# Splitting the operands of both head sums one stage ahead of their products

## The chip, the cores and the metric

The kernel runs on one core of one Trainium2 chip. The metric is the time of one execution on the device, in microseconds (us); of several runs the median is given. TensorE multiplies matrices (PE in the profile; PEld is its weight load), VectorE (DVE), ScalarE (ACT) and GpSimd (POOL) work elementwise, and SyncE (SP) issues the DMAs. Each engine takes its instructions in one fixed order, written when the program is built; an instruction that waits holds up everything behind it on its engine.

## What is computed

One layer over 1024 tokens of width 1024: a retention mixer (4 heads) and an RWKV-7 mixer (8 heads of 64 channels) read one projection; then come an output projection, a gated FFN, an embedding gate and a norm. The change touches two sums over the 64 channels of an RWKV head:

```python
kk = k * k_k.reshape(H, N)
kk = kk * lax.rsqrt(jnp.maximum(jnp.sum(kk * kk, axis=-1, keepdims=True), 1e-24))
k = k * (1.0 + (a - 1.0) * k_a.reshape(H, N))
...
bonus = jnp.sum(r * k * r_k, axis=-1, keepdims=True) * v
return (y + bonus.reshape(B, S, W)) * g
```

## The kernel before

Channels lie on the partitions and tokens run along the free dimension, in two halves of 512 tokens. The dense layers are long rows of 128x512 matmuls (tile `d` and, in the tail, `pd` and `pg`). Each fp32 operand is split into two parts, `hi` (rounded on ACT, L250) and `lo` (the rest, subtracted on DVE or POOL, L251), and a product is hi by hi, hi by lo and lo by hi.

The RWKV mixer works on eight groups: four pairs of heads, p0 to p3, for the first half of the tokens and then again for the second. A group (`rwkv_group`) goes through the stages prep, ops, A, tok, mid, chain, fin and done. `weave` writes the program: whenever the dense matmuls written so far are worth the wait that a stage has asked for, it writes the group's next step, and otherwise one more piece of the dense layer. A group enters tok when the group before is in fin, so the two run beside each other. A list scheduler then fixes each engine's order: by the order of writing where it can, and later where an operand or a buffer is not yet free by its reckoning.

The steps that matter here:

- prep squares k times its weight into `kk2`; ops sums it over the channels with two matmuls against a block of ones (tile `ss`).
- A makes `kp` (r times k times a weight, L615), the masked products `pb`, and a chain of 62 small DVE instructions on `tmp` and `R` (L646, L648: 31 pairs, shapes 128x8x31 down to 128x8x1) that inverts a triangular block. That chain is called the inversion here.
- tok makes two sets of `pk` products and from them `aak` on DVE (L668), sums `kp` over the channels (tile `bo`, L672), multiplies the sum by v into `bv` (L674), and transposes five operands on PE (tile `pq`, four transposes each), each set copied out by four ACT copies (L685).
- fin of the group before transposes `Y` into `py`, normalises it on DVE into `yn` (L779) and transposes back (`pyt`). L784 adds `bv`.

`headsum` splits its operand into a tile `hs` pair and multiplies in one go. Its `hi` half takes one of the two buffers of tag "f" (HBUF = 2), which `Y` and `yn` of the group before use as well; its `lo` half takes one of the five of tag "t". The PSUM tiles `ss`, `bo`, `pq`, `pk`, `pb` and `pS` share the two banks of `psa`.

Of the kernel before, what the change touches and what calls it, by code (L numbers as in the profile page):

```python
# [178 lines left out]
def tile_hybrid_layer(ctx: ExitStack, tc: tile.TileContext, I, out):  # L179
# [7 lines left out]
    def mm(ps, lhsT, rhs, start, stop, more=False):  # L187
        n = math.prod(rhs.shape[1:])
        pe[0] += n / 2.4 if rhs.dtype == F32R else 2 * max(107.0, n / 1.2)
        m = nc.tensor.matmul(ps, lhsT, rhs, start=start, stop=stop, skip_group_check=more)  # L190
        tail["mm"] = m.ins
        return m
# [22 lines left out]
    def K(n):  # L215
        return cst[:, _C[n][0]:_C[n][1]]
# [4 lines left out]
    def pv(i):  # L221
        return par[:, i:i + 1]
# [3 lines left out]
    def psa(name):  # L226
        return psr.tile([P, 512], F32, tag="ra", name=name, bufs=2)

    def psq(name):
        return psd.tile([P, 512], F32, tag="d", name=name)  # L230
# [3 lines left out]
    def pse(name):  # L234
        tag = ("ra", "rc", "ra", "rm", "rt")[npx[0] % 5]
        npx[0] += 1
        return psr.tile([P, 512], F32, tag=tag, name=name, bufs=2 if tag == "ra" else 1)
# [11 lines left out]
    def split(src, hi, lo, eng=None):  # L249
        act(hi, src, AF.Copy)  # L250
        return (eng or V).tensor_tensor(out=lo, in0=src, in1=hi.bitcast(F32), op=ALU.subtract)  # L251
# [101 lines left out]
    with ExitStack() as s1:  # L353
# [194 lines left out]
        def v3(t):  # L548
            return t.rearrange("p (u t) -> p u t", t=C)

        def flat(t):
            return t.rearrange("p h t -> p (h t)")
# [3 lines left out]
        def rwkv_group(p, hf):  # L556
# [6 lines left out]
            def tt2(name):  # L563
                return t2.tile([P, HS], F32, tag="t", name=name)
# [1 line left out]
            def tf(name):  # L566
                return t2.tile([P, HS], F32, tag="f", name=name, bufs=HBUF)

            def headsum(ps, t):

                hi, lo = (t2.tile([P, HS], F32R, tag=HTAG[i], name="hs", bufs=(HBUF, 5)[i]) for i in range(2))
                split(t, hi, lo)
                mm(ps, onesr, hi, start=True, stop=False)
                mm(ps, onesr, lo, start=False, stop=True)

# [2 lines left out]
                dma(out=t, in_=lowd[4 * i + p, :, tok])  # L578
            kk2 = tt2("kk2")
            act(kk2, k, AF.Square, scale=pv(KK + p))  # L580
            yield "prep", PREPW

            ss = psa("ss")
            headsum(ss, kk2)
            behind = tc.issue_after(invs[-1]) if invs else nullcontext()
            with behind:
                V.tensor_scalar(out=th, in0=th, scalar1=1.0, scalar2=None, op0=ALU.add)
# [23 lines left out]
            kp = tt2("kp")  # L611
# [47 lines left out]
            XR = rp.tile([P, NU, 2, C], F32, tag="XR", name="XR")  # L659
            KA = rp.tile([P, NU, 2, C], F32, tag="KA", name="KA", bufs=KAB)  # L660
            aak = v3(tt2("aak"))
            for g in range(2):
                us = slice(4 * g, 4 * g + 4)
                pk = psa("pk")
                for u in range(4):
                    mm(pk[:, u * P:(u + 1) * P], flat(kabd[:, 4 * g + u]), AR[:, :, 4 * g + u, :], start=True, stop=True)
                pkv = pk.rearrange("p (u x t) -> p u x t", u=4, x=2)
                V.tensor_tensor(out=aak[:, us, :], in0=pkv[:, :, 0, :], in1=K("mak").unsqueeze(1).broadcast_to([P, 4, C]), op=ALU.mult)  # L668
                V.tensor_tensor(out=KA[:, us, 1, :], in0=pkv[:, :, 1, :], in1=mincl4, op=ALU.mult)
                yield "tok", 900  # L670
            bo = psa("bo")
            headsum(bo, kp)  # L672
            bv = t2.tile([P, HS], F32, tag="bv", name="bv", bufs=1)
            V.tensor_tensor(out=bv, in0=bo, in1=v, op=ALU.mult)  # L674
            SG = t2.tile([P, HS], F32, tag="sg", name="sg", bufs=1)
# [14 lines left out]
            for h in range(2):  # L690
                lo, up = slice(C * h, C * h + 32), slice(C * h + 32, C * h + C)
# [51 lines left out]
            for u in range(NU):  # L743
# [5 lines left out]
                if hf == 0 or u < NU - 1:  # L749
# [3 lines left out]
                    ps = psa("pS")[:, 0:P]  # L753
# [543 lines left out]
        for h in range(2):  # L1297
            for k in range(KT):
                tasks[f"mix{h}{k}"] = (mix_load(h, k), 0, ["wo0" if h else "x0free", f"ret{k}{h}" if k < 4 else f"group{k - 4}{h}"])
        weave([(f"group{p}{hf}", rwkv_group(p, hf), need[p]) for hf in range(2) for p in range(4)],  # L1300
              tasks, dg, count, pe, done)

# [142 lines left out]
    for a, b in passes:  # L1445
        h, n = a // HS, b - a
        t = slice(a - h * HS, b - h * HS)
        for d in range(KT):
# [9 lines left out]
            ps = psq("pg")[:, 0:n] if a < HS else pse("pg")[:, 0:n]  # L1458
# [86 lines left out]
```

## Time and profile before

| | |
|---|---|
| median of 3 runs | 1598.35 us (1597.43 to 1599.26) |
| the profiled execution, its own time | 1598.74 us |
| its span, first to last instruction | 1597.0 us |
| PE, DVE, ACT, POOL busy | 94%, 75%, 45%, 32% of the span |
| mean granted TensorE clock | 0.986 of 2.4 GHz |
| chain that ended last, by engine | PE 57%, DVE 23%, ACT 7%, DMA 6% |

The span is the stretch that the trace shows; the time of the run lies 1.74 us above it. The chain that ended last is followed back from the last instruction, at each step to what released it. The groups of the RWKV mixer lie between about 75 and 915 us; the FFN's second half and the embedding gate come after them.

### The profile page before, as it was taken

The page shows a single profiled execution, that of the slowest core. Times are in us where ns is not written, and L with a number is a line of the kernel's source. Part 1 is how long each engine was busy: PE and PEld are TensorE (multiplying, and loading weights), DVE is VectorE, ACT ScalarE, POOL GpSimd, SP SyncE. Part 2 cuts the span into 40 slices and gives each one's busy share as a digit, 9 for nine tenths or more (in the row PEclk, how much of TensorE's full clock was granted, in tenths as well). Part 3 has the DMA queues.
Part 4 walks back from the last instruction along what each step waited for, and adds up shares of the span by engine and source line. Part 5 has one row for each costly group of instructions (what it writes and reads, how often), then busy time and mean ns, then how long its engine had stood idle before and what let it go on. Part 6 is the DMA issues. An engine that isn't in the chain of part 4 may idle for free.

```text
span 1597.0 us, 21675 instructions
## 1 busy us (share of the span) xinstructions
PE 1497.2 (94%) x7328; PEld 1220.0 (76%) x7328; DVE 1203.1 (75%) x2466; ACT 722.4 (45%) x1442; POOL 512.7 (32%) x389
## 2 busy tenths in 40 slices
PE   6999899998888889989889999999999999999997
PEld 5777768776677767767768877778888888888897
DVE  7668895969889696894875545768888888886675
ACT  6755435353545647445344324543333333334554
POOL 7411111121321122324223340455555555570000
PEclk9999999999999999999999999999999999999998
DMA  6544242242544555335233546332223222331222
GB/s 199 175 154 166 96 129 84 89 152 78 174 133 145 189 165 190 96 105 155 87 127 113 171 119 188 115 121 85 92 90 90 91 93 86 119 93 56 83 91 75
DMA packets 108767, 194.09 MB, mean 122 GB/s; under 512 B 12272, under 2 KB 16496, under 8 KB 108656
## 3 DMA queue, kind: packets, MB, share of 16 engines
q1 hardware_dynamic: 108656, 192.71, 38.0%
q8 instruction: 58, 0.95, 0.2%
q14 instruction: 53, 0.43, 0.1%
HBM read 151.24 MB, written 41.42 MB: 121 GB/s over the span
## 4 chain that ended last, share of the span: by engine, by line
PE 57%; DVE 23%; ACT 7%; DMA 6%; issue 4%; POOL 2%; SPq 0%; ACTq 0%; DVEq 0%; POOLq 0%
PE d L190 31%; PE pd L190 13%; PE pg L190 6%; DVE tmp L646 4%; DVE R L648 3%; DMA st<-in_w_gate_dram 2%; POOL lo L251 2%; DMA st<-in_w_up_dram 1%; DVE lo L251 1%; ACT hi L250 1%; DVE Dm L640 1%; DVE inv L599 1%; PE pkh L190 1%; PE pb L190 1%; ACT BA L685 1%
## 5 line engine op out<-in xcount | busy, mean ns | idle before, releaser
L190 PE MATMUL d<-hT,hi 128*128 128x512 f32 x1408 | 452.0, 401 | 4.1 <-ACT hi L250 4.1
L251 POOL TENSOR_TENSOR lo<-st,hi 128x512 fp32r<-128x512 f32 x173 | 241.8, 1399 | 590.6 <-ACT hi L250 531.3
L190 PE MATMUL d<-x,hi 128*128 128x512 f32 x960 | 319.7, 408 | 8.9 <-ACT x L339 8.0
L190 PEld LDWEIGHTS d<-hT,hi 128*128 128x128 f32 x1408 | 263.5, 192 | 54.9 <-ACT hi L250 5.6
L250 ACT ACTIVATE hi<-st 128x512 fp32r<-128x512 f32 x298 | 187.0, 628 | 258.2 <-PE d L190 96.4
L190 PE MATMUL d<-hT,lo 128*128 128x512 f32 x704 | 279.8, 398 | 5.9 <-DVE lo L251 3.4
L190 PE MATMUL pd<-ring 128*128 128x512 f32 x948 | 260.4, 389 | 0.0
L190 PEld LDWEIGHTS d<-x,hi 128*128 128x128 f32 x960 | 177.1, 192 | 43.3 <-ACT x L339 8.0
L190 PEld LDWEIGHTS pd<-ring 128*128 128x128 f32 x948 | 177.9, 188 | 37.1 <-ACT rm L1145 0.2
L190 PE MATMUL d<-x,lo 128*128 128x512 f32 x480 | 192.9, 402 | 2.8 <-POOL lo L251 2.4
L190 PEld LDWEIGHTS d<-hT,lo 128*128 128x128 f32 x704 | 134.2, 191 | 38.3 <-DVE lo L251 6.3
L251 DVE TENSOR_TENSOR lo<-st,hi 128x512 fp32r<-128x512 f32 x125 | 115.7, 927 | 55.9 <-ACT hi L250 54.9
L1147 DVE TENSOR_TENSOR x<-x,pd 128x512 f32<-128x512 f32 x180 | 118.6, 679 | 26.9 <-PE pd L190 26.9
L251 POOL TENSOR_TENSOR ring<-xr,ring 128x512 fp32r<-128x512 f32 x53 | 73.2, 1386 | 146.5 <-ACT ring L250 67.3
L250 ACT ACTIVATE ring<-rm 128x512 fp32r<-128x512 f32 x87 | 53.8, 629 | 131.3 <-DVE rm L1080 83.8
L190 PEld LDWEIGHTS d<-x,lo 128*128 128x128 f32 x480 | 92.0, 192 | 23.1 <-POOL lo L251 4.7
L646 DVE TENSOR_TENSOR tmp<-Dt,R 128x248 f32<-128x248 f32 (+30 forms) x248 | 89.5, 361 | 3.2
L648 DVE TENSOR_TENSOR R<-R,tmp 128x248 f32<-128x248 f32 (+30 forms) x248 | 83.8, 338 | 3.3
L190 PE MATMUL d<-mix,hi 128*128 128x512 f32 x256 | 82.1, 400 | 0.9 <-ACT hi L250 0.9
L251 DVE TENSOR_TENSOR ring<-rm,ring 128x512 fp32r<-128x512 f32 x65 | 58.4, 902 | 13.0 <-ACT ring L250 12.1
L250 ACT ACTIVATE ring<-xr 128x512 fp32r<-128x512 f32 x57 | 34.9, 625 | 73.8 <-PE pd L190 72.6
L190 PEld LDWEIGHTS d<-mix,hi 128*128 128x128 f32 x256 | 48.1, 192 | 10.8 <-ACT hi L250 1.3
(315 smaller groups left out, 2393.7 us busy)
## 6 DMA issues: line engine op xcount, KB each, us to landing
st<-in_w_gate_dram SPq DMA_DIRECT2D x88, 256.0 KB, 2.9
st<-in_w_up_dram SPq DMA_DIRECT2D x88, 256.0 KB, 2.9
st<-in_w_in_dram SPq DMA_DIRECT2D x86, 256.0 KB, 2.9
xr<-in_w_down_dram SPq DMA_DIRECT2D x44, 256.0 KB, 2.7
retd<-rt SPq DMA_DIRECT2D x32, 256.0 KB, 2.5
rr<-retd SPq DMA_DIRECT2D x32, 256.0 KB, 3.4
st<-in_w_o_dram SPq DMA_DIRECT2D x32, 256.0 KB, 3.0
rkvd<-rkvt SPq DMA_DIRECT2D x24, 256.0 KB, 2.1
```

What stands on the lines that cost most here:

```text
L190: m = nc.tensor.matmul(ps, lhsT, rhs, start=start, stop=stop, skip_group_check=more)
L250: act(hi, src, AF.Copy)
L251: return (eng or V).tensor_tensor(out=lo, in0=src, in1=hi.bitcast(F32), op=ALU.subtract)
L599: V.reciprocal(out=inv, in_=inv)
L640: V.tensor_tensor(out=Dm, in0=d0v[:, 0].rearrange("p u t -> p t u").unsqueeze(2).broadcast_to([P, 32, 4, NU]), in1=d0v[:, 1].rearrange("p ...
L646: V.tensor_tensor(out=tmp[:, :, 0:i], in0=Dt[:, i:i + 1, 0:i].broadcast_to([P, 8, i]), in1=R[:, :, i:i + 1].broadcast_to([P, 8, i]), op=AL ...
L648: V.tensor_tensor(out=R[:, :, 0:i], in0=R[:, :, 0:i], in1=tmp[:, :, 0:i], op=ALU.subtract)
L685: act(dst(h)[h * C:(h + 1) * C, j::2, :], pqv[j * C:(j + 1) * C, :, h, :], AF.Copy)
L1147: V.tensor_tensor(out=dst, in0=dst, in1=ps, op=ALU.subtract if name == "P4" else ALU.add)
```

## The change

`headsum` is cut in two. `headparts` allocates the two halves and splits; `headsum` only multiplies. The split of `kk2` is written at the end of prep instead of in ops, and the split of `kp` at the beginning of tok, ahead of the two sets of `pk`, instead of behind them. No operation is added or taken away.

```diff
-            def headsum(ps, t):
-
+            def headparts(t):
                 hi, lo = (t2.tile([P, HS], F32R, tag=HTAG[i], name="hs", bufs=(HBUF, 5)[i]) for i in range(2))
                 split(t, hi, lo)
+                return hi, lo
+
+            def headsum(ps, hi, lo):
+
                 mm(ps, onesr, hi, start=True, stop=False)
                 mm(ps, onesr, lo, start=False, stop=True)
...
             act(kk2, k, AF.Square, scale=pv(KK + p))
+            kk2 = headparts(kk2)
             yield "prep", PREPW
 
             ss = psa("ss")
-            headsum(ss, kk2)
+            headsum(ss, *kk2)
...
             aak = v3(tt2("aak"))
+            kp = headparts(kp)
             for g in range(2):
...
             bo = psa("bo")
-            headsum(bo, kp)
+            headsum(bo, *kp)
```

The scheduler turns this into other orders. Lines below the edit carry numbers that are 3 to 5 higher in the changed kernel. On PE, in tok of p1 in the first half, the order before has the transposes of the group before first and the sum and the five sets behind them:

```order
L196 MATMUL pyt<-cst,yn 128x128 x4
L190 MATMUL d<-x_98,hi 128x512 x2
L190 MATMUL d<-x_98,lo 128x512
L190 MATMUL d<-x_98,hi 128x512
L190 MATMUL bo<-hs,onesr 128x512
L196 MATMUL pq<-cst,aak 128x128 x4
L190 MATMUL d<-x_98,hi 128x512
L190 MATMUL d<-x_98,lo 128x512
L190 MATMUL bo<-hs,onesr 128x512
L190 MATMUL d<-x_98,hi 128x512 x2
L190 MATMUL d<-x_98,lo 128x512
L196 MATMUL pq<-cst,v 128x128 x4
```

In the changed kernel the sum comes nine dense matmuls behind the second set of `pk`, and the transposes of the group before come 36 dense matmuls after it, as before at the 681st dense matmul of the program:

```order
L190 MATMUL pk<-AR,kabd 128x128 x4
...
L190 MATMUL bo<-hs,onesr 128x512 x2
L190 MATMUL d<-x_98,hi 128x512 x2
L190 MATMUL d<-x_98,lo 128x512
L190 MATMUL d<-x_99,hi 128x512
L196 MATMUL pq<-cst,aak 128x128 x4
L190 MATMUL d<-x_99,hi 128x512
L190 MATMUL d<-x_99,lo 128x512
...
L196 MATMUL pyt<-cst,yn 128x128 x4
L196 MATMUL pq<-cst,AR 128x128 x4
```

So `bo` and four of the five `pq` sets moved ahead of `pyt`. Counted in dense matmuls, `bo` moves forward by 40, 54, 36, 51, 52, 49 and 49 in the seven groups that follow another; in the first group it stays. The `pq` sets move by 18 to 52. They now stand 4 to 19 dense matmuls behind `bo` and mostly 6 to 12 apart from each other (`aak` of p1 in the second half stands right behind `bo`). `pyt` itself stays where it was, or stands 9 to 13 dense matmuls earlier in three groups and 6 later in one.

On ACT, at the same place, the first fence is before and the second is the change. `Y` belongs to the group before, `hs<-kp` is the `hi` half, and L685 or L690 are the copies out of `pq`:

```order
L763 ACTIVATE Y<-pZ 128x4x64
L756 ACTIVATE Sn<-pS,PC 128x128
L250 ACTIVATE hi<-st 128x512 x2
L250 ACTIVATE hs<-kp 128x512
L685 ACTIVATE XR<-pq 64x4x64 x4
L580 ACTIVATE kk_2244<-k,par 128x512
L250 ACTIVATE hs<-kk_2244 128x512
```

```order
L768 ACTIVATE Y<-pZ 128x4x64
L250 ACTIVATE hs<-kp 128x512
L761 ACTIVATE Sn<-pS,PC 128x128
L756 ACTIVATE STb<-pZ 64x64
L250 ACTIVATE hi<-st 128x512
...
L690 ACTIVATE KA<-pq 64x4x64 x4
L250 ACTIVATE hs<-kk_2244 128x512
L690 ACTIVATE XR<-pq 64x4x64 x4
```

The rounding of `kp` moved from behind both `Y` copies to between them, and the rounding of the next group's `kk2` moved back behind the fourth set of `pq` copies.

On DVE, at the same place, `hs<-kp` is the `lo` half. Before, it stood behind the end of the inversion:

```order
L784 SCALAR_TENSOR_TENSOR Y<-pyt,par,bv 128x512
L652 COPY Xd<-tmp 128x256
L251 TENSOR_TENSOR hs<-kp,hs 128x512
L654 STREAM_TRANSPOSE R<-Xd 128x256
L785 SCALAR_TENSOR_TENSOR Y<-Y,par,sg 128x512
L674 TENSOR_TENSOR bv<-bo,v 128x512
```

In the changed kernel it stands inside the inversion, at its twelfth pair of 31:

```order
L650 TENSOR_TENSOR tmp<-Dt,R 128x8x21
L652 TENSOR_TENSOR R<-R,tmp 128x8x21
L650 TENSOR_TENSOR tmp<-Dt,R 128x8x20
L251 TENSOR_TENSOR hs<-kp,hs 128x512
L652 TENSOR_TENSOR R<-R,tmp 128x8x20
```

`bv` stays behind `Y<-pyt` (L784, now L789), because it has one buffer and that instruction reads the old one.

## Rows read from the trace of the kernel before

**Rows 1.** The page's first part: busy us, share of the span, instructions.

```profile
PE 1497.2 (94%) x7328; PEld 1220.0 (76%) x7328; DVE 1203.1 (75%) x2466; ACT 722.4 (45%) x1442; POOL 512.7 (32%) x389
```

**Rows 2.** Busy time by stretch: us, PE, PEld, DVE, ACT, POOL; clock, DMA.

```profile
60.00:960.00 900.00, 828.00 (x4235) 663.88 (x4234) 676.98 (x1717) 418.87 (x927) 221.12 (x170) 0.98 0.42 134
400.00:500.00 100.00, 87.75 (x472) 69.62 (x471) 87.50 (x244) 47.85 (x110) 24.96 (x18) 0.98 0.46 147
```

**Rows 3.** Waits of PE over the span: total us, times, longest us.

```profile
PE pS L196 <- DVE STb L752: 18.2, 22, 1.7
...
PE bo L190 <- DVE hs L251: 4.9, 3, 2.3
...
PE pyt L196 <- DVE yn L779: 1.9, 2, 1.0
PE pyt L196 <- DVE R L648: 1.8, 1, 1.8
PE pq L196 <- ACT Vbd L685: 1.6, 4, 0.6
...
PE pq L196 <- ACT BA L685: 1.5, 6, 0.4
PE ss L190 <- ACT KA L685: 1.4, 3, 0.5
...
PE bo L190 <- ACT hs L250: 1.3, 1, 1.3
...
PE pq L196 <- ACT XR L685: 0.5, 2, 0.3
```

**Rows 4.** Tile hs: ns min/median/max, first and last start; idle time before it.

```profile
L250 ACT ACTIVATE hs<-kp x8: 613/632/635, 110.2 to 816.6; 128x512 fp32r<-128x512 f32 x8
L251 DVE TENSOR_TENSOR hs<-kp,hs x8: 641/685/1762, 130.2 to 817.3; 128x512 fp32r<-128x512 f32 x8
...
  PE pyt L196: 12.2, 5
```

**Rows 5.** Timeline of ACT, p1, first half: start, us, instruction, [idle before <-releaser].

```profile
230.07 0.64 ACT L250 ACTIVATE hs<-kp 128x512 fp32r<-128x512 f32 x1 [4.01 <-PE pyt L196]
...
234.58 1.55 ACT L685 ACTIVATE Vbd<-pq 64x256 f32<-64x256 f32 x4
```

**Rows 6.** Timeline of PE, p1, second half.

```profile
592.84 0.63 PE L196 MATMUL pyt<-cst,yn 128*128 128x128 f32 x4 [1.03 <-DVE yn L779]
593.23 0.71 PE L190 MATMUL d<-mix,hi 128*128 128x512 f32 x2
...
595.66 0.50 PE L190 MATMUL bo<-hs,onesr 128*128 128x512 f32 x1 [1.26 <-ACT hs L250]
...
598.73 0.80 PE L190 MATMUL bo<-hs,onesr 128*128 128x512 f32 x1 [2.13 <-DVE hs L251]
```

**Rows 7.** Busy time by stretch, columns as in rows 2.

```profile
597.30:604.10 6.80, 5.37 (x15) 4.20 (x16) 4.66 (x8) 4.51 (x9) 0.00 (x0) 0.50 0.75 222
```

**Rows 8.** Timeline of DVE, p1, first half.

```profile
210.08 0.33 DVE L646 TENSOR_TENSOR tmp<-Dt,R 128x160 f32<-128x160 f32 x1
```

**Rows 9.** Timeline of PE at the same place: the first set of pk.

```profile
213.59 1.05 PE L190 MATMUL pk<-AR,kabd 128*128 128x128 f32 x8
```

**Rows 10.** Chain that ended last: start, us, what (six dense matmuls).

```profile
357.41 1.38 PE d L190 x6
```

**Rows 11.** Timeline of DVE: the second aak of p1 first, p2 second half.

```profile
220.44 0.40 DVE L668 TENSOR_TENSOR aak<-pk,cst 128x256 f32<-128x256 f32 x1
...
690.79 0.41 DVE L668 TENSOR_TENSOR aak<-pk,cst 128x256 f32<-128x256 f32 x1
```

**Rows 12.** Timeline of PE: dense matmuls beside the first of these.

```profile
219.96 0.62 PE L190 MATMUL d<-x,hi 128*128 128x512 f32 x2
```

**Rows 13.** Timeline of PE, p2 of the second half.

```profile
692.51 0.88 PE L190 MATMUL rY<-rr 128*128 128x128 f32 x4 [2.74 <-DVE rmisc L859]
```

**Rows 14.** Timeline of DVE, p1, second half: the second pb.

```profile
553.18 0.49 DVE L634 TENSOR_TENSOR d<-pb,cst 128x128 f32<-128x128 f32 x2 [8.72 <-PE pb L190]
```

**Rows 15.** Timeline of PE, p3, second half: two sets of transposes of the retention.

```profile
812.52 1.12 PE L196 MATMUL rtp<-cst,rr 128*128 128x128 f32 x4 [4.21 <-ACT rr L829]
```

## Prediction

> **What bounds the kernel now.** I begin with the page's first part [rows 1]: PE is busy 94% of the span, so a change that adds and removes no operation can only win or lose idle time of PE (or time in which its clock is down). The windows say where that idle time lies [rows 2]: from 60 to 960 us, where the eight groups of the RWKV mixer run beside dense matmuls, PE is busy 828.00 of 900 us, that is, 72 us idle. Behind that stretch the change moves no instruction. In the worst stretches DVE is as full as PE (87.50 of 100 us against 87.75), so DVE work that comes later there can hold PE up.
>
> The waits of PE [rows 3] then say on whom it waits: mostly on DVE's `STb` in the chain stage (`pS`, 18.2 us in 22 waits), which the change doesn't touch, and in the rows shown of tok and fin on `hs` (`bo`: 4.9 and 1.3 us), on `yn` and `R` (`pyt`: 1.9 and 1.8 us), and on the ACT copies of a set (`pq`: 1.6, 1.5 and 0.5 us; `ss`: 1.4 us).
>
> Why `bo` waits is seen in the tile `hs` and in two timelines. The `hi` half for `kp` takes a buffer of tag "f" that `yn` of the group before holds until `pyt` has read it. So ACT stands idle before it until `pyt`, 12.2 us in five groups [rows 4], 4.01 us of it in p1 of the first half [rows 5]. Only then comes `lo` on DVE, behind other work. In p1 of the second half PE waits 1.26 us for `hi` and 2.13 us for `lo` [rows 6], and straight behind that the granted clock is 0.50, the 1.2 GHz level, for 6.80 us, in which PE is busy 5.37 us [rows 7].
>
> **The change, part by part.** The sum is made against the profiled execution, 1598.74 us (0.39 us above the median of the runs).
>
> *The waits of `bo`.* In the changed order of p1 in the first half, `lo` stands behind the `tmp` that starts at 210.08 us [rows 8], and lasts about 0.69 us. `hi` takes 0.63 us on ACT [rows 4] and stands ahead of the second copy of `Y`, so it must be there by then too. `bo` is written behind both sets of `pk`, the first of which ran at 213.59 us [rows 9]. By these rows both halves are ready more than 2 us before PE can ask. Gain: 4.9 + 1.3 = 6.2 us, all of it.
>
> *The waits of `pyt`.* In most groups `pyt` keeps its place among the dense matmuls, but now `bo` and four sets of `pq` lie ahead of it. A set takes 0.39 us of PE [rows 6], `bo` some 0.5 us, so PE gets there about 2.1 us later relative to DVE. That covers the longest waits of 1.8 and 1.0 us in part or whole; I take 2.4 of the 3.7 us.
>
> *The waits between sets.* Four ACT copies of one set take 1.55 us [rows 5]; a dense matmul takes 1.38 / 6 = 0.23 us [rows 10]. The sets now stand mostly 6 to 12 dense matmuls, 1.4 to 2.8 us, apart, so that the copies mostly keep up. Of 1.6 + 1.5 + 0.5 = 3.6 us I take three quarters, 2.7. The wait of `ss` behind such copies, 1.4 us, goes because the sets are long over when `ss` comes.
>
> *The clock.* The lowered stretch of [rows 7] followed the waits of `bo`, 1.26 + 2.13 us within 4 us. Without them I take it to stay at 2.4 GHz: half of 5.37 us, 2.7 us. Whether the waits caused it, no row shows; the bounds are 0 and 2.7.
>
> Gains: 6.2 + 2.4 + 2.7 + 1.4 + 2.7 = 15.4 us.
>
> *New waits.* `lo` now takes its 0.69 us of DVE inside the inversion, ahead of `aak`, and nothing on DVE leaves that stretch in exchange. Before, the second `aak` of p1 in the first half ended at 220.44 + 0.40 = 220.84 us [rows 11], and PE was among dense matmuls from 219.96 to 220.58 us [rows 12]. Now `aak` ends near 221.5 us, and the set `pq<-aak`, moved to stand behind four or five dense matmuls after `bo`, is asked for at about 220.6 us. That is a wait of about 0.9 us; in p2 of the second half (690.79 us [rows 11]) it is as tight. I price it at 0.7 us (one `lo`) in five groups: 3.5 us. The bounds: 0, if DVE has room to catch up, as in p1 of the second half, where it stood 8.72 us waiting for `pb` [rows 14] and that set now comes earlier; and 2.74 us a time, the wait of PE on a late DVE in p2 of the second half [rows 13]. I lie nearer to the low end because the cause of the wait is one instruction of 0.7 us. What is queued behind a waiting `pq` on PE is the dense row and the next set; ACT's copies wait for that.
>
> In three groups `pyt` stands 9 to 13 dense matmuls earlier (2.1 to 3.0 us), about as much as the work that came ahead of it, while `yn` is 0.7 us later; in p2 and p3 of the first half I add 0.85 us each: 1.7 us.
>
> *Edits at nothing.* The split of `kk2` in prep: its rounding on ACT stands behind the fourth set of copies instead of beside them, and ACT is 45% busy. What covers it is the dense row between prep and `ss`. If that cover is short, `ss` waits one rounding and one subtraction, 0.63 + 0.69 = 1.3 us, a group. In some groups that rounding still needs the buffer that `pyt` frees; so ACT's 12.2 us shrink but don't vanish, and what is late next is the copies of the fifth set behind it. `bv` keeps its place; `bo` then holds a PSUM bank longer, which the other sets can do without as they go through the second bank. The bounds of this are 0 and 1.3 us a group; I take 0.
>
> Sum: 15.4 − 3.5 − 1.7 = 10.2 us, 1598.74 − 10.2 = **1588.5 us**.
>
> **A rule weighed.** The `lo` for `kp` takes 685 ns in the median, but 1762 ns once [rows 4]: something else held that one up for 1.08 us. The Trainium skill (SBUF — State Buffer, "Who interferes with whom") gives a cause: VectorE's second read port is shared with GpSimd as an exclusive lock, so a subtraction of two SBUF operands is blocked by a GpSimd instruction that reads SBUF. That would speak against putting it in a stretch where GpSimd is busy. By the trace, seven of eight were not held, and GpSimd is busy 221.12 of 900 us here [rows 2], so I leave the sum as it is and keep the lock as rival E.
>
> **The rivals.**
>
> *B. More is won.* PE comes into the later stages at other times relative to ACT and DVE. In p3 of the second half it waited 4.21 us for `rr` [rows 15]; if the five sets and `bo` lie ahead of that wait instead of behind it, most of it is filled. With the new waits (5.2 us) half gone as well: 1588.5 − 4.2 − 2.6 = 1581.7, and with another lowered stretch like that of [rows 7] avoided, 1.7 to 2.7 more: about 1580 us. Against it: `rr` and the dense rows around it keep their order.
>
> *C. No change.* DVE sets the pace where it is busy 87.50 of 100 us; it does the same work, and what PE wins in tok it gives back at the next `pS`. The 18.2 us there [rows 3] would grow by about 10. Time: about 1598 us. For it: `STb` is by far the largest wait. Against it: PE is just as full, and from 60 to 960 us DVE has 223 us free.
>
> *D. Slower.* `pq<-aak` stands too early: DVE is later than I reckon, PE waits in each of five groups as long as in [rows 13], 2.74 us, and loses to a lower clock behind it some 1.7 us (half of a stretch half as long as that of [rows 7]). That is 5 × 4.44 = 22.2 us in place of the 3.5 us of the sum: 1598.74 + 22.2 + 1.7 − 15.4 = 1607.2 us. It decides where the new waits at `pq` and `pyt` average over 15.4 / 7 = 2.2 us in each group that follows another. For it: the sets moved up by 18 to 52 dense matmuls while `aak` didn't get earlier on DVE. Against it: what precedes `aak` on DVE grew by a single instruction.
>
> *E. The subtraction is held.* In all seven moved groups `lo` takes the 1762 ns, 1.08 us more: 7.5 us on a DVE that leads to `aak`, `R` and `yn`. If three quarters of it reaches PE, 5.7 us, the time is 1588.5 + 5.7 = 1594.2 us. This is what that page's lock would do at its worst; this case's rows show it once in eight.
>
> *The change does nothing* can't be: the orders differ in every group after the first.
>
> **How the numbers follow.** Chances: the sum as reckoned 0.46 (its own range 1582 to 1594), B 0.12, C 0.18, D 0.16, E 0.08. The likeliest gives 1588.5 us. What this kernel's measurement can tell from no change is about 0.2%, 3.2 us: faster is below 1595.2, slower above 1601.5. The first case, B and E end below: 0.46 + 0.12 + 0.08 = 0.66; C within: 0.18; D above: 0.16. The range leaves out D and what of B lies beyond its estimate: 1579 to 1601 us, with about 0.2 outside.
>
> **What would show it right or wrong.** Right: no wait of PE on `hs` at `bo`; `hi` for `kp` on ACT without idle time until `pyt`; no lowered clock in p1 of the second half near 590 us; the wait of DVE for the second `pb` there gone; waits of `pq` on `aak` below 1 us each; PE's idle time from 60 to 960 us down from 72 to about 60 us. Wrong on the side of D: waits of `pq<-aak` of 2 us or more, with lowered clock behind them. On the side of C: `bo` without waits, but `pS` on `STb` well above 18.2 us. On the side of E: a median of `lo` near 1.7 us. The forecast also fails if `pyt` asks for `yn` so much earlier that its waits pass 3.7 us, or if `ss` now waits for its early split.

## The result and the profile after

The changed kernel takes 1592.16 us (median of 8 runs, 1587.93 to 1595.94) against 1602.54 us for the kernel before in runs beside it: a ratio of 0.9942 (95% interval 0.9922 to 0.9962), or 9.3 us less; the two medians are 10.4 us apart. The profiled execution took 1588.42 us, with a span of 1586.6 us against 1597.0. The forecast was 1588.5 us, 10.2 us less.

The page's first part reads nearly as in [rows 1]: the engines do the same work in a shorter span.

```profile
PE 1490.3 (94%) x7328; PEld 1218.7 (77%) x7328; DVE 1210.2 (76%) x2466; ACT 719.9 (45%) x1442; POOL 516.1 (33%) x389
```

The window that answers to the first of [rows 2] runs here from 59.51 to 942.51 us, between the same two PE instructions (`low<-rr` and `ryt`) that stood at 60.82 and 951.49 us before. Columns are as in [rows 2].

```profile
59.51:942.51 883.00, 815.26 (x4192) 657.16 (x4190) 677.96 (x1713) 413.45 (x923) 222.38 (x167) 0.98 0.42 135
```

PE is idle 883.00 − 815.26 = 67.7 us of it, where it was 72.0 us. Now the waits of PE, to be held against [rows 3] (total us, times, longest us):

```profile
PE pS L196 <- DVE STb L757: 18.9, 24, 2.3
...
PE ryt L196 <- ACT rr L876: 8.1, 3, 3.8
...
PE pq L196 <- ACT XR L690: 3.6, 6, 2.1
...
PE pq L196 <- DVE R L652: 2.2, 1, 2.2
PE pq L196 <- DVE KA L674: 1.6, 3, 0.9
...
PE bo L190 <- DVE KA L674: 0.7, 2, 0.5
...
PE ss L190 <- DVE hs L251: 0.6, 1, 0.6
PE pq L196 <- DVE tmp L650: 0.6, 1, 0.6
PE pq L196 <- ACT KA L690: 0.6, 2, 0.3
PE pq L196 <- ACT Vbd L690: 0.5, 2, 0.3
PE pq L196 <- ACT BA L690: 0.5, 2, 0.2
```

No wait of `bo` on `hs` is left and none of `pyt`. In their place stand waits of `pq` on DVE (2.2 + 1.6 + 0.6 = 4.4 us, one each in five groups), a longer wait of `pq` on ACT, and a longer one of the retention's `ryt`. The tile `hs` answers to [rows 4]: ACT no longer stands idle ahead of it until `pyt`.

```profile
L250 ACT ACTIVATE hs<-kp x8: 621/624/632, 108.8 to 779.3; 128x512 fp32r<-128x512 f32 x8
L251 DVE TENSOR_TENSOR hs<-kp,hs x8: 680/685/1759, 122.4 to 780.3; 128x512 fp32r<-128x512 f32 x8
...
  DVE hs L251: 1.7, 2
```

Where the time went is best seen by taking the same PE instruction in both traces and subtracting the starts (before minus after). Each column stands at such an instruction; its head is the start in the kernel before.

| us | 201 | 289 | 374 | 462 | 540 | 645 | 665 | 773 | 883 | 951 | 1587 |
|---|---|---|---|---|---|---|---|---|---|---|---|
| lead of the changed kernel | 1.31 | 3.63 | 6.24 | 8.91 | 8.77 | 9.99 | 13.44 | 8.95 | 8.96 | 8.99 | 9.62 |

The first 1.31 us arise before 61 us, ahead of any moved PE instruction, and 0.6 us after 951 us, where the orders are the same: those are the two executions, not the change. Of the rest, p1, p2 and p3 of the first half bring 2.3, 2.6 and 2.7 us, p1 of the second half 4.7 us (from 540 to 665 us), and p2 of the second half gives 4.5 us back.

### The profile page after: what moved, and what is told of

Its sections match the earlier page's. It is cut to its first block, busy times and chain, and to the rows that moved or that the text cites. A ratio compares the mean times of both kernels' runs of the same rounds, so it can differ in the third digit from the quotient of the medians.

```text
span 1586.6 us, 21684 instructions
## 1 busy us (share of the span) xinstructions
PE 1490.3 (94%) x7328; PEld 1218.7 (77%) x7328; DVE 1210.2 (76%) x2466; ACT 719.9 (45%) x1442; POOL 516.1 (33%) x389
## 4 chain that ended last, share of the span: by engine, by line
PE 63%; DVE 23%; DMA 5%; ACT 4%; issue 3%; POOL 2%; SPq 0%; DVEq 0%; ACTq 0%; POOLq 0%
PE d L190 36%; PE pd L190 14%; PE pg L190 6%; DVE tmp L650 3%; DVE R L652 3%; POOL lo L251 1%; DVE lo L251 1%; DVE Dm L644 1%; DVE inv L603 1%; PE pb L190 1%; DMA st<-in_w_up_dram 1%; DMA st<-in_w_gate_dram 1%; ACT hi L250 1%; PE pq L196 1%; PE pkh L190 1%
## 5 line engine op out<-in xcount | busy, mean ns | idle before, releaser
L652 DVE TENSOR_TENSOR R<-R,tmp 128x248 f32<-128x248 f32 (+30 forms) x248 | 87.4, 352 | 3.7
L650 DVE TENSOR_TENSOR tmp<-Dt,R 128x248 f32<-128x248 f32 (+30 forms) x248 | 84.2, 339 | 3.4
```

The costliest lines, as they stand in the source:

```text
L650: V.tensor_tensor(out=tmp[:, :, 0:i], in0=Dt[:, i:i + 1, 0:i].broadcast_to([P, 8, i]), in1=R[:, :, i:i + 1].broadcast_to([P, 8, i]), op=AL ...
L652: V.tensor_tensor(out=R[:, :, 0:i], in0=R[:, :, 0:i], in1=tmp[:, :, 0:i], op=ALU.subtract)
```

## The experiments

Ratios are to the kernel before, in runs beside each.

**Which half of the change.** `e1_kp_only` takes back the split of `kk2`:

```diff
-            kk2 = headparts(kk2)
             yield "prep", PREPW
 ...
-            headsum(ss, *kk2)
+            headsum(ss, *headparts(kk2))
```

> The changed kernel with the split of kk2 back in ops; only the split of kp stays early. Theory 1 (the whole gain comes from the split of kp, because PE no longer stands at bo and the pq sets come ahead of pyt): ratio to the kernel before 0.994 +- 0.002, PE's waits at bo below 1 us in all. Rival 2 (the early split of kk2 carries part of it, over ss and ACT): a ratio of 0.996 to 0.998. Rival 3 (most of the difference is run to run): 1.000.

Measured: 0.9934 (0.9916 to 0.9952). The orders on PE, ACT, DVE and POOL are those of the changed kernel, so the place where the split of `kk2` is written changes nothing there, and this run measures the same order a second time. PE waits 0.7 us at `bo`.

`e2_kk2_only` takes back the split of `kp`:

```diff
-            kp = headparts(kp)
             for g in range(2):
 ...
-            headsum(bo, *kp)
+            headsum(bo, *headparts(kp))
```

> The changed kernel with the split of kp back behind the two sets of pk; only the split of kk2 is early. PE's order is that of the kernel before. Theory 1: ratio 1.000 +- 0.001, the waits at bo as before, 6.2 us. Rival 2: 0.996 to 0.998, with the 1.4 us of ss gone and the idle time of ACT changed.

Measured: 1.0000 (0.9986 to 1.0014). Its waits of PE are those of [rows 3] again:

```profile
PE bo L190 <- DVE hs L251: 4.3, 4, 2.1
PE bo L190 <- ACT hs L250: 2.1, 2, 1.3
PE pyt L196 <- DVE yn L783: 2.0, 2, 1.1
PE pyt L196 <- DVE R L652: 1.8, 1, 1.8
```

So the gain comes with the split of `kp`; that of `kk2` brings nothing that these runs can tell (within 0.14%). Rivals 2 and 3 fall.

**Why bo was late.** `e3_before_rbuf` leaves the writing as it was and only gives the `hi` half of `kp` another buffer, that of `r`, which is free by then:

```diff
-            def headsum(ps, t):
+            def headsum(ps, t, tag="f", bufs=HBUF):
 ...
-            headsum(bo, kp)
+            headsum(bo, kp, "r", 1)
```

> The kernel before, with the split of kp where it was, but its hi half in the buffer of r (no longer needed there) instead of one that yn of the group before holds. In PE's order bo then moves forward by 35 to 56 dense matmuls without any change of the writing. Theory 1 in its narrow form (bo is late because hi has to wait for the buffer of yn; where the split is written does not matter): 0.994 to 0.996, ACT's idle time of 12.2 us before hi gone. Rival 4 (the place of the split is what counts): 0.999 to 1.001.

Measured: 0.9944 (0.9925 to 0.9963), the gain of the change within the noise. The scheduler now moves the split by itself. In the tile `hs` ACT's idle time until `pyt`, 12.2 us in [rows 4], is down to one wait:

```profile
L250 ACT ACTIVATE hs<-kp x8: 615/631/633, 109.0 to 727.7; 128x512 fp32r<-128x512 f32 x8
...
  PE pyt L196: 0.8, 1
```

So the cause is the buffer shared with `yn`. Writing the split earlier works because it then takes a buffer ahead of `yn`. The way there is not the same in every term: in this run `pq` waits 8.3 us on DVE, where the changed kernel waits 4.4.

`e4_before_bo_last` moves the sum and `bv` behind the five sets instead:

```diff
-            bo = psa("bo")
-            headsum(bo, kp)
-            bv = ...
 ...                                  (the five pq sets)
+            bo = psa("bo")
+            headsum(bo, kp)
+            bv = ...
```

> The kernel before, with the sum over kp and bv written behind the five pq sets instead of ahead of them; nothing is split earlier. In PE's order the sets come forward as in the changed kernel, and bo comes behind pyt by 5 to 15 dense matmuls. If the gain is in the sets having come forward and bo no longer standing ahead of them: 0.994 to 0.997. If it needs bo's operands early: bo waits again, 4 us or more, and the ratio is 0.998 to 1.001.

Measured: 0.9984 (0.9970 to 0.9998). The sets come forward, but `bo` waits again, in its waits of PE for 8.8 + 2.2 us, and the sets' first transposes wait for `aak`:

```profile
PE bo L190 <- DVE hs L251: 8.8, 4, 3.1
...
PE pq L196 <- DVE aak L668: 5.8, 6, 1.8
...
PE bo L190 <- ACT XR L681: 2.2, 1, 2.2
```

That is the second case. Moving the sets forward alone is worth little (0.16%); the operands of `bo` must be there too.

**Which groups.** The split of `kp` is early in one half of the tokens only, or everywhere but in p2 of the second half. The diff is that of e5; e6 has `hf == 1` in the same places, e7 and e11 `(p, hf) != (2, 1)`:

```diff
-            kp = headparts(kp)
+            if hf == 0:
+                kp = headparts(kp)
 ...
-            headsum(bo, *kp)
+            headsum(bo, *(kp if hf == 0 else headparts(kp)))
```

> The split of kp is early in the four groups of the first half of the tokens only. By the trace of the changed kernel PE's lead over the kernel before grows by 2.3, 2.6 and 2.7 us in p1, p2 and p3 of the first half. Theory A (the groups add up): 1600 - 7.6, ratio 0.995. Theory B (what PE is ahead in the first half is given back in the second, where DVE is late): 0.997 to 1.000, with a lead of 8 us at 460 us that shrinks after it.

Measured: 0.9962 (0.9946 to 0.9978), between the two theories.

> The split of kp is early in the four groups of the second half of the tokens only. In the changed kernel the lead grew there by 4.7 us up to p2 and lost 4.5 us in p2. Theory A (the loss belongs to p2's own edit): nothing in sum, 0.999 to 1.000. Theory B (the loss comes from a lead that PE brings along from the first half): the 4.7 us stay, 0.997.

Measured: 0.9971 (0.9955 to 0.9987), the time of theory B.

> The changed kernel, but in p2 of the second half the split of kp stays behind the two sets of pk. Theory A (the early split itself costs 4.5 us there, since pq<-aak then waits for DVE): those are won, ratio 0.991. Theory B (PE meets later work of DVE and ACT anyway when it is ahead): as the changed kernel, 0.994.

Measured: 0.9930 (0.9911 to 0.9950), 1586.72 us. Since this lies between the two theories, it was run again beside the changed kernel:

> The changed kernel again, as the measure for the two runs beside it: 0.994.

> The kernel with the late split in p2 of the second half again, beside the changed kernel on one chip. Theory A (the early split costs 4.5 us in that group): 3 to 5 us below the changed kernel. Theory B (PE meets later work there anyway): within 1.5 us of it.

Measured: the changed kernel 0.9953 (0.9936 to 0.9970), 1592.22 us; with the late split in that group 0.9929 (0.9911 to 0.9946), 1588.22 us. The lead in the profiled executions, at instructions as in the table above:

| us | 201 | 462 | 665 | 773 | 1587 |
|---|---|---|---|---|---|
| changed kernel | 1.3 | 8.9 | 13.4 | 9.0 | 9.6 |
| changed kernel again (e10) | 0.4 | 8.1 | 10.2 | 7.0 | 5.3 |
| e5, first half only | 0.2 | 7.1 | 6.8 | 5.6 | 4.3 |
| e6, second half only | 1.0 | 1.8 | 9.2 | 6.3 | 6.1 |
| e7, late split in p2 of the second half | 0.5 | 7.7 | 10.4 | 12.4 | 14.0 |
| e11, the same again | 0.5 | 6.8 | 9.4 | 8.1 | 7.5 |
| e8, lo twice | 2.5 | 3.9 | 4.1 | 2.7 | 0.5 |
| e9, lo on POOL | 1.2 | 0.3 | 2.4 | −0.9 | −4.8 |
| e12, no lo | 2.2 | 7.3 | 14.5 | 12.0 | 11.4 |

The halves add up within their intervals: 0.38% + 0.29% = 0.67% against 0.58% and 0.47% together. A lead brought along from the first half is not simply lost in the second. In p2 of the second half (665 to 773 us) the kernels that split early there lose 2.5 to 4.5 us (e8, which has little lead, 1.4), and e5, which doesn't, loses 1.2 us. e6 has the time of theory B but not its account: it loses 2.8 us there with hardly a lead from the first half, and its time comes from the stretch up to 665 us, where it gains 7.4 us from 462 us on. With the late split the stretch loses 1.2 us (e11) or gains 2.0 us (e7): two executions of the same kernel, 3.2 us apart.

That speaks for theory A in its direction, but not for its 4.5 us. The 4.0 us between the medians of e10 and e11 are the most that the runs give. The same order as the changed kernel gave 0.9942, 0.9953 and, in e1, 0.9934, and the late split in that group 0.9930 and 0.9929; by these ratios they lie 0.6 to 4 us apart, and the intervals overlap. So some gain is likely, and its size is not shown.

What the late split changes in PE's waits came out alike in e7 and e11. The 2.2 us of `pq` on DVE in that group are gone, and those of `ryt` are 5.1 and 5.2 us where the changed kernel has 8.1 us, and 8.0 us again in e10: one wait of some 3.7 us is gone. In return a wait of 2.7 us at `rY` comes back, `bo` waits 2.1 us for `hs` and `pq` 1.1 us for `bv`. By these waits the two ways cost about the same, 5.9 us each. In e11:

```profile
PE rY L190 <- DVE rmisc L865: 5.6, 6, 2.7
PE ryt L196 <- ACT rr L877: 5.2, 2, 3.8
```

**What lo costs.** `e8_lo_twice` writes the subtraction of `kp` a second time (kp0 is the unsplit tile):

```diff
             kp = headparts(kp)
+            V.tensor_tensor(out=kp[1], in0=kp0, in1=kp[0].bitcast(F32), op=ALU.subtract)
```

> The changed kernel with the lo subtraction of kp done twice on DVE, 0.69 us more in each of eight groups, 5.5 us in all: the term of the new waits, doubled. If DVE has room (new waits as priced, 0.7 us in five groups): 3.5 us more than the changed kernel, ratio 0.996. If DVE is the second bound there: 5 us or more, 0.997 and above. If the new waits cost nothing: 0.994.

Measured: 0.9991 (0.9977 to 1.0006). Against the three measurements of the changed order, 0.9934 to 0.9953, that is 6 to 9 us more for 8 × 0.68 = 5.5 us of DVE: the second case. The scheduler moved more than that one instruction, though. On PE most of what moved did so by less than 15 dense matmuls, but the `pb` of one group moved by 42 to 46 and four matmuls of `pw` by 93. So the 6 to 9 us are the price of the subtraction together with this other order.

`e9_lo_pool` gives it to GpSimd:

```diff
-            def headparts(t):
+            def headparts(t, eng=None):
 ...
-                split(t, hi, lo)
+                split(t, hi, lo, eng)
 ...
-            kp = headparts(kp)
+            kp = headparts(kp, G)
```

> The changed kernel with the lo subtraction of kp on GpSimd instead of VectorE: 0.69 us of DVE less in each group inside the inversion. Doubling that instruction cost about 7 us. Theory D (DVE is the second bound there, and each lo costs PE about 1 us a group): ratio 0.989 to 0.991. Rival (GpSimd's subtraction takes 1.3 us or more and holds DVE's instructions up meanwhile, or bo is then waited for): 0.994 or above.

Measured: 0.9990 (0.9975 to 1.0005): the rival; `bo` is not waited for (0.5 us). The timelines of DVE and of POOL at p1 of the first half show one of the eight places:

```profile
208.91 0.33 DVE L650 TENSOR_TENSOR tmp<-Dt,R 128x160 f32<-128x160 f32 x1
209.27 1.35 DVE L652 TENSOR_TENSOR R<-R,tmp 128x160 f32<-128x160 f32 x1
```

```profile
209.16 1.29 POOL L251 TENSOR_TENSOR hs<-kp,hs 128x512 fp32r<-128x512 f32 x1 [1.47 <-ACT hs L250]
```

`R` begins 0.11 us after POOL's subtraction, and ends at 210.62 us, 0.17 us after POOL's end at 210.45. The `tmp` of the same size ahead of it took 0.33 us. DVE lost 1.02 us to an instruction that was taken off it to spare 0.69.

`e12_no_lo` does without the subtraction:

```diff
-            kp = headparts(kp)
+            kp_hi = t2.tile([P, HS], F32R, tag="f", name="hs", bufs=HBUF)
+            act(kp_hi, kp, AF.Copy)
+            kp = (kp_hi, kp_hi)
```

> The changed kernel without the lo subtraction of kp: the sum over kp adds the hi half a second time in its place, so PE does as many products as in the changed kernel, and the bonus it forms is not the reference's. With e8 this makes a series of no, one and two subtractions of 0.69 us on DVE in each group. If each costs PE about as much as the second one did (7 us in all): ratio 0.990. If the first one is mostly covered (3.5 us as priced in the prediction): 0.992. If PE gains nothing: 0.994 to 0.995.

Measured: 0.9925 (0.9906 to 0.9944), near the second case. The orders on PE, ACT and DVE are those of e9, so the 10 us between e9 and e12 (0.9990 against 0.9925) come from the eight subtractions on GpSimd and their effects alone. DVE executes the same 2458 instructions in both, and is busy 12.6 us longer in e9. The first part of the two pages, e9 first:

```profile
PE 1499.7 (94%) x7328; PEld 1226.7 (77%) x7328; DVE 1213.9 (76%) x2458; ACT 721.7 (45%) x1442; POOL 523.8 (33%) x397
PE 1494.5 (94%) x7328; PEld 1223.7 (77%) x7328; DVE 1201.3 (76%) x2458; ACT 721.3 (45%) x1442; POOL 512.2 (32%) x389
```

At each of the eight places a DVE instruction begins beside the subtraction, takes 0.45 to 1.10 us longer than the same instruction in e12 (7.5 us in all), and ends 0.01 to 0.19 us after it.

No, one and two subtractions on DVE give 0.9925, 0.9934 to 0.9953 and 0.9991: by the ratios the first costs 1 to 4.5 us and the second 6 to 9 us. The interval of e12 overlaps those of the changed order, and e8 and e12 each have an order of their own, so this is no clean series, and that the second costs more than the first is likely, not shown.

## Why the prediction was right, and where not

The time, the sign and the mechanism of the gain came out: `bo` was late because of the buffer that `yn` held (e3), and the gain is that of the `kp` half (e1, e2). New waits of `pq` on DVE came too, but they end with another instruction than the one reckoned with. The size came out partly by terms that cancel and partly by luck. By the rows of waits:

| term | forecast, us | measured, us |
|---|---|---|
| `bo` | −6.2 | −5.5 (0.7 left, on `KA`) |
| `pyt` | −2.4 and +1.7 | −3.7, none left |
| `pq` behind ACT's copies | −2.7 | +1.6 (3.6 to 5.2) |
| `ss` | −1.4 | −0.8 (0.6 left, on its early split) |
| clock | −2.7 | about 0 |
| new waits on DVE at `pq` | +3.5 | +4.4 |
| sum | −10.2 | −4.0 |

PE's idle time fell by 72.0 − 67.7 = 4.3 us, close to the last line, since the other waits that changed nearly cancel: `rtp` is gone with its 4.21 us [rows 15], `ryt` rose from 4.8 to 8.1 us, the dense rows wait longer for their own splits, and `rY` less for DVE. The rest of the 10.4 us between the two spans is 3.4 us by which PE is busy for less time (818.67 us before between the same instructions, 815.26 now) and 2.7 us outside this stretch. Neither was in the sum, which has 10.2 us where the waits give 4.0: that the total came so near is in good part luck. Some of the shorter busy time is seen at `bo`: in [rows 6] its two matmuls, each behind a wait, are busy 0.50 and 0.80 us, and now the two together 0.62 us. What the rest comes from is not settled. Of the signs that the prediction named, PE's idle time was to fall to about 60 us and is 67.7, the wait of DVE for the second `pb` in p1 of the second half did shrink from 8.72 to 0.50 us, and `ss` does wait once for its split, 0.6 us; e1, with that split written late, has the same wait.

*`bo`.* In p1 of the first half the margin of `lo` was as reckoned or better. The timelines of DVE and PE there:

```profile
209.02 0.69 DVE L251 TENSOR_TENSOR hs<-kp,hs 128x512 fp32r<-128x512 f32 x1
...
218.91 0.38 DVE L673 TENSOR_TENSOR aak<-pk,cst 128x256 f32<-128x256 f32 x1
...
219.45 0.41 DVE L674 TENSOR_TENSOR KA<-pk,cst 128x256 f32<-128x256 f32 x1
```

```profile
217.88 0.62 PE L190 MATMUL bo<-hs,onesr 128*128 128x512 f32 x2
...
220.01 0.63 PE L196 MATMUL pq<-cst,aak 128*128 128x128 f32 x4 [0.61 <-DVE tmp L650]
```

`lo` is ready 8 us before `bo` asks. The new wait of the first set is 0.61 us where 0.9 was worked out, but that is luck. `aak` ended at 218.91 + 0.38 = 219.29 us, before PE had come to the set at 219.40 us. What ended last was `KA` at 219.86 us, 0.15 us ahead of the set. By the kernel, `KA` is the last to read the second `pk`, and with `bo` in the one of the two `psa` banks the set needs the bank of that `pk`. So by the order of these ends the bank decides here, and not the operand; the prediction did not reckon with `KA`. In e4, where no `bo` stands ahead, the first sets do wait for `aak`.

*The waits between sets: the step that failed.* 2.7 of 3.6 us were to go, because the copies would keep up with sets that stand 6 to 12 dense matmuls apart; 5.2 us are there now. The copies of one set do take 1.55 us. But the term that the prediction put at nothing, `bo` holding a PSUM bank longer, is not nothing. In p2 of the first half, where the sets stand four to six dense matmuls apart, the timelines of PE and DVE show:

```profile
309.31 0.66 PE L196 MATMUL pq<-cst,bk 128*128 128x128 f32 x4 [0.25 <-ACT Vbd L690]
...
311.60 0.66 PE L196 MATMUL pq<-cst,bk 128*128 128x128 f32 x4 [0.25 <-ACT BA L690]
...
313.90 0.66 PE L196 MATMUL pq<-cst,AR 128*128 128x128 f32 x4 [0.27 <-ACT KA L690]
```

```profile
314.69 0.65 DVE L679 TENSOR_TENSOR bv<-bo,v 128x512 f32<-128x512 f32 x1
```

Each set waits for the copies of the set right before it (`Vbd`, `BA` and `KA` in the order of the sets), since `bv` reads `bo` only after the last set and all five go through the one bank that is left. In all seven groups `bv` begins after the last set. In the kernel before, `bv` came earlier and the later sets took turns: in p1 of the first half the second `bk` waited for `Vbd`, two sets back. Its timeline of PE has:

```profile
236.18 0.66 PE L196 MATMUL pq<-cst,bk 128*128 128x128 f32 x4 [0.36 <-ACT Vbd L685]
```

Eleven such waits of 0.2 to 0.5 us make 3.1 of the 5.2 us. That a second buffer for `bv` would free the bank, and what it would bring, was not tried.

The twelfth is 2.13 us, and there the prediction had treated ACT as free to start the copies. In p1 of the second half the timelines of PE and of ACT show:

```profile
580.16 0.66 PE L196 MATMUL pq<-cst,v 128*128 128x128 f32 x4 [2.13 <-ACT XR L690]
```

```profile
577.43 0.72 ACT L339 ACTIVATE hT<-rr,par 128x512 fp32r<-128x512 f32 x1 [2.62 <-DVE rr L990]
578.06 0.61 ACT L317 ACTIVATE rr<-rr 128x512 f32<-128x512 f32 x1
578.58 1.53 ACT L690 ACTIVATE XR<-pq 64x256 f32<-64x256 f32 x4
```

ACT waited 2.62 us for DVE with an instruction of the dense layer that stands ahead of the copies `XR` of the set before; the moved set pays for it. What is queued ahead of the copies on ACT, and which bank each set takes, should have been read from the order.

*The clock.* The stretch of [rows 7] began while `bo` still stood in its second wait, which ended at 598.73 us, and not behind it. It is gone: PE runs at full clock there now. But others came, such as the one behind `ryt` in the window 701.30 to 704.70 us and one at 465.70 us:

```profile
701.30:704.70 3.40, 3.09 (x10) 2.61 (x11) 3.40 (x6) 2.03 (x5) 0.00 (x0) 0.51 0.81 225
465.70:469.10 3.40, 3.40 (x11) 2.49 (x10) 3.34 (x15) 1.38 (x4) 0.00 (x0) 0.50 0.00 0
```

Such pieces add up to some 27 us between 60 and 960 us in either profile, and PE is busy 25.8 us of them before and 26.8 us now. The 2.7 us were a gain at one place that was paid at another; the mean granted clock of that part is 0.98 in both.

*The new waits.* 4.4 us in five waits against 3.5 in five groups, but half of it is one wait, in p2 of the second half, beyond the limit of 1 us each that was given. There the mechanism of rival E is at work. The timelines of PE, DVE and POOL:

```profile
677.79 0.63 PE L196 MATMUL pq<-cst,aak 128*128 128x128 f32 x4 [2.16 <-DVE R L652]
...
701.61 1.12 PE L196 MATMUL ryt<-cst,rr 128*128 128x128 f32 x4 [3.76 <-ACT rr L876]
```

```profile
665.44 1.76 DVE L251 TENSOR_TENSOR hs<-kp,hs 128x512 fp32r<-128x512 f32 x1
...
668.08 1.11 DVE L650 TENSOR_TENSOR tmp<-Dt,R 128x144 f32<-128x144 f32 x1
...
671.92 1.34 DVE L652 TENSOR_TENSOR R<-R,tmp 128x120 f32<-128x120 f32 x1
...
676.68 0.41 DVE L673 TENSOR_TENSOR aak<-pk,cst 128x256 f32<-128x256 f32 x1
...
677.23 0.42 DVE L674 TENSOR_TENSOR KA<-pk,cst 128x256 f32<-128x256 f32 x1
```

```profile
665.37 1.28 POOL L1012 TENSOR_TENSOR g<-g,R 128x512 f32<-128x512 f32 x1 [1.49 <-DVE g L1011]
667.74 1.28 POOL L251 TENSOR_TENSOR lo<-st,hi 128x512 fp32r<-128x512 f32 x1 [1.09 <-ACT hi L250]
671.84 1.28 POOL L251 TENSOR_TENSOR lo<-st,hi 128x512 fp32r<-128x512 f32 x1 [2.82 <-ACT hi L250]
```

The set starts 0.14 us after the end of `KA`, which follows `aak`. Three times before `aak` a DVE instruction begins beside one of POOL and ends only after it, by 0.14 to 0.55 us: the moved `lo` among them, 1.76 us in place of 0.69. The Trainium skill (SBUF — State Buffer, "Who interferes with whom") says that a VectorE instruction with two SBUF inputs contends with a GpSimd instruction that reads SBUF, for a shared port pair under an exclusive lock. The rows agree: 667.74 + 1.28 = 669.02 us ends POOL's subtraction, and 668.08 + 1.11 = 669.19 us ends the `tmp` beside it. In the forecast this was one in eight, and it is still one in eight for `lo`, in the same group as before the change; now PE asks for the set soon after. It is a part of the wait at most, since without the subtraction (e12) the set still waits 1.8 us there. The wait of `ryt` 24 us later belongs to the early split in this group: of the kernels here, all that split early there have it (3.6 to 4.4 us), e12 without `lo` among them, and e5, e7 and e11 do not. Which instruction on the way delays it is open.

*Rivals.* C and D fall by the result. D's wait exists (2.16 us in p2 of the second half) but in one group, not five. B's `rtp` wait of 4.21 us [rows 15] is gone, as B said, while `ryt` took 3.3 us more. The gain that rival C would give back at `pS` is 0.7 us (18.2 to 18.9).

*The price of lo.* The prediction took 0.7 us for each late `aak` and 3.5 us in all; leaving the subtraction out wins 1 to 4.5 us (e12). That does not show the price to be right: in e12 the waits of `pq` on DVE are 3.8 + 2.2 + 1.0 = 7.0 us, more than the 4.4 of the changed kernel, so what e12 wins lies elsewhere, in an order of its own. That `lo` makes these waits is argued and not shown.

## What to carry to other kernels

When an operand's split comes late, look first at who holds its buffer: a tag shared with the stage before can tie two stages together, and another buffer (e3) or an earlier allocation of the same one brings the same gain. Work that moves forward on PE inherits whatever is queued ahead of its copies on ACT and ahead of its operands on DVE, so read the orders of those engines at the new place, group by group, and ask which PSUM bank is still held there. The one group where that was worse is likely better left as it was (e11: 4.0 us below the changed kernel by medians, less against e1). Two profiled executions of kernels that differ nowhere yet can stand 1.3 us apart at 61 us, so judge a change by the lead gained between two places, not by the spans.

## What was not expected of the hardware

Taking a subtraction off VectorE and giving it to GpSimd made the kernel 6 to 9 us slower, as much as doing it twice on VectorE. GpSimd takes 1.29 us for it where VectorE takes 0.69, and a small VectorE instruction that met it took 1.35 us where the same instruction without the neighbour (e12) took 0.32. At the eight places VectorE's instructions lost 7.5 us to the neighbour, where 8 × 0.69 = 5.5 us were spared.
